# An encoder trunk on one core: x ahead in the loads, c as 48 fp32r rows, a remade opening

## The chip, the cores and the metric

The program runs on one core of a Trainium2 chip. The metric is the device time of one execution in microseconds, as the median of several runs. Engines in the profile: PE is TensorE (matmul), PEld its weight loads, DVE is VectorE, ACT is ScalarE, POOL is GpSimd, and SP issues DMAs.

## The reference

There are two layers over x (256 tokens by 1024). Each has a token mixer (grouped-query attention with axial rotary positions, three groups of dilated attention, two gates) and a squared-ReLU MLP. A vector c of 1024 values sets shift, scale and gate of both sublayers in each layer:

```
c_act = silu(c)
for l in range(2):
    ada = c_act @ w_ada[l] + b_ada[l]           # (6 * 1024): sh1 sc1 gt1 sh2 sc2 gt2
    h = rms(x, g_mix[l]) * (1 + sc1) + sh1
    parts = h @ w_in[l]                          # q, k, v of four attentions, two gates
    ...                                          # rope, attentions, branches
    x = x + gt1 * (mixed @ w_out[l])
    h2 = rms(x, g_mlp[l]) * (1 + sc2) + sh2
    x = x + gt2 * (square(relu(h2 @ w_ff1[l])) @ w_ff2[l])
```

All of it is f32. Weights come to about 180 MB in all.

## The kernel before

Each large matrix product is made from fp32r matmuls in one pass. A weight tile of 128 x 1024 (512 KB) lands in `wr`; ACT copies it, rounded to fp32r, into the first half of `w`, and DVE subtracts to give the low part (`split_next`). Activations are split likewise (`hT` and others), and three matmuls (high by high, low by high, high by low) give one product: `mm3` and `many`. A plain f32 matmul is two recorded PE instructions.

The ada vectors don't use PE. DVE multiplies a 128 x 1024 tile of the transposed `w_ada` by `c_act`, which holds silu(c) on every partition, and reduces along the row: `ada_tile`, 96 times. Bias and gain follow as small DVE instructions (`sh_sc`, `first_sh_sc`, and the first one in `gt_row`).

**How the order is set.** The program records all operations in a class `Plan`, with a cost for each. A list scheduler (`run`) places them: PE's recorded order gives the due times, the other engines work backward from these, and the scheduler picks the most urgent operation that is ready on each engine. The result is a fixed order for each engine. `CFG` holds the order of the mixers' pieces (`seq0`, `seq1`: a and b are the attentions, c a qkv chunk, u and v gates, y a branch, w one ada tile), how many ada tiles go between the MLP's pieces (`ada_f0`), and which first chunk is finished first (`post0`). Constants such as `COLD`, `FIRST` and `FETCH` model start-up and transfers.

**The opening.** SP issues c (as a zero-padded block of 128 rows with an 8 x 8 identity beside it), then in the order of `OPEN["loads"]` the first half of x (`x0`, with an identity matrix, all biases and gains and half the rotary table), `x1`, two w_ada tiles and the two first weight tiles `wx` and `wy`. `OPEN["steps"]` names the steps in PE's order: C (silu of c, then eight f32 matmuls with a broadcast column, which put c on all partitions), X (sum of squares, GpSimd's power, scaling, transposes into `xT`), T (rotary tables by matmul), A (the first shift and scale), H (the first `hT`), W (a split), M (the matmuls of k = 0 for one pair of column chunks and one half of the rows), F (warm matmuls on zeros). `plain` names the pairs done by f32 matmuls without a split of h; a weight tile whose two halves are both plain isn't split at all. `eng` says whether ACT or DVE makes each copy. After this k = 1 to 7 follow, each with two ada tiles, `hT` for that k, and 24 matmuls into the same eight PSUM banks.

The diff touches lines 32 to 64 (the constants), 240 to 680 (the planner), 745 to 840 (tiles on chip, ada) and 1586 to 1770 (the opening), and the layout of the inputs from 1824 on.

## Time and profile before

| | us |
|---|---|
| median of 3 runs | 724.97 (724.77 to 725.4) |
| the profiled execution | 725.12 |
| its span, first to last instruction | 723.3 |
| PE busy | 718.4 |
| weight loads busy | 597.2 |
| DVE busy | 587.6 |
| ACT busy | 466.3 |
| POOL busy | 69.6 |

The mean granted clock of TensorE over the span is 1.00. Matmuls are pipelined, and their ends are modelled: two neighbours overlap in the table of times, so the pace of a stretch is read from the distance of the starts, or from the count of matmuls in a stage. All operations are issued from one helper line, L721, so the groups are told apart by their tiles. In brackets behind a row stands the idle time of its engine just before it, and what ended it.

### The profile page before, as it was taken

The page shows a single profiled execution, that of the slowest core. Times are in us where ns is not written, and L with a number is a line of the kernel's source. Part 1 is how long each engine was busy: PE and PEld are TensorE (multiplying, and loading weights), DVE is VectorE, ACT ScalarE, POOL GpSimd, SP SyncE. Part 2 cuts the span into 40 slices and gives each one's busy share as a digit, 9 for nine tenths or more (in the row PEclk, how much of TensorE's full clock was granted, in tenths as well). Part 3 has the DMA queues.
Part 4 walks back from the last instruction along what each step waited for, and adds up shares of the span by engine and source line. Part 5 has one row for each costly group of instructions (what it writes and reads, how often), then busy time and mean ns, then how long its engine had stood idle before and what let it go on. Part 6 is the DMA issues. An engine that isn't in the chain of part 4 may idle for free.

```text
span 723.3 us, 10610 instructions
## 1 busy us (share of the span) xinstructions
PE 718.4 (99%) x3860; PEld 597.2 (83%) x3860; DVE 587.6 (81%) x919; ACT 466.3 (64%) x791; POOL 69.6 (10%) x60
## 2 busy tenths in 40 slices
PE   9999999999999999999999999999999999999998
PEld 6788888788888888888888888878788888888887
DVE  6999999999999986594799999797899755456643
ACT  7569678965764766653565598658848766545640
POOL 0007640000100040000032201010000000000000
PEclk9999999999999999999999999999999999999999
DMA  9998668997499997596565687967376965576101
GB/s 349 408 401 270 193 203 295 348 373 243 142 350 406 381 359 278 183 325 233 175 221 207 213 328 269 338 226 280 122 258 199 344 207 159 172 229 211 52 0 59
DMA packets 50868, 180.95 MB, mean 250 GB/s; under 512 B 5728, under 2 KB 6784, under 8 KB 50816
## 3 DMA queue, kind: packets, MB, share of 16 engines
q1 hardware_dynamic: 50816, 180.28, 70.7%
q8 instruction: 30, 0.49, 0.3%
q14 instruction: 22, 0.18, 0.1%
HBM read 178.66 MB, written 1.06 MB: 248 GB/s over the span
## 4 chain that ended last, share of the span: by engine, by line
PE 98%; DMA 1%; SPq 0%; issue 0%; DVE 0%
PE ps L721 98%; DMA wr<-in_w_y 1%; SPq L721 0%; DVE xin L721 0%
## 5 line engine op out<-in xcount | busy, mean ns | idle before, releaser
L721 DVE TENSOR_TENSOR w<-wr,w 128x1024 fp32r<-128x1024 f32 x234 | 282.3, 1229 | 44.7 <-ACT w L721 44.3
L721 ACT ACTIVATE w<-wr 128x1024 fp32r<-128x1024 f32 x234 | 241.5, 1056 | 81.8 <-PE ps L721 38.9
L721 PE MATMUL ps<-w,hT 128*128 128x512 f32 x1032 | 246.4, 395 | 0.0
L721 PEld LDWEIGHTS ps<-w,hT 128*128 128x128 f32 x1032 | 190.3, 188 | 41.5 <-DVE hT L721 1.7
L721 PE MATMUL ps<-w,hid 128*128 128x512 f32 (+1 forms) x780 | 176.0, 385 | 0.0
L721 PEld LDWEIGHTS ps<-w,hid 128*128 128x128 f32 x780 | 143.1, 188 | 28.3
L721 PE MATMUL ps<-hT,w 128*128 128x512 f32 (+1 forms) x896 | 158.5, 337 | 0.0
L721 PEld LDWEIGHTS ps<-hT,w 128*128 128x128 f32 x896 | 139.4, 190 | 18.7
L721 DVE CUSTOM_DVE_ANT_0 s2k<-wr,c_act 128x1024 bf16<-128x1024 f32 x96 | 116.1, 1227 | 0.0
L721 ACT ACTIVATE s2k<-ps 128x256 f32<-128x256 f32 (+3 forms) x108 | 45.4, 440 | 81.0 <-PE ps L721 75.3
L721 DVE TENSOR_TENSOR s2k<-ps,s2k 128x256 f32<-128x256 f32 x56 | 22.8, 419 | 32.5 <-ACT s2k L721 32.5
L721 PE MATMUL ps<-w,mT 128*128 128x512 f32 x192 | 45.6, 393 | 0.0
L721 ACT ACTIVATE s2k<-s2k 128x512 f32<-128x512 f32 (+1 forms) x62 | 38.6, 623 | 9.2 <-DVE s2k L721 8.3
L721 PEld LDWEIGHTS ps<-w,mT 128*128 128x128 f32 x192 | 35.5, 188 | 7.4 <-ACT mT L721 0.2
L721 POOL TENSOR_TENSOR rstd<-rstd,half 128x8 f32<-128x8 f32 (+1 forms) x20 | 30.1, 1509 | 87.8 <-DVE rstd L721 87.7
L721 POOL TENSOR_TENSOR ss<-ss,half 128x1 f32<-128x1 f32 x8 | 11.1, 1383 | 261.7 <-DVE ss L721 254.6
L721 DVE TENSOR_TENSOR hid<-s2k,hid 128x512 fp32r<-128x512 f32 x28 | 20.1, 719 | 19.8 <-ACT hid L721 19.7
L721 ACT ACTIVATE pr<-pr,st 128x256 f32<-128x256 f32 (+1 forms) x64 | 32.3, 558 | 0.8 <-DVE st L721 0.8
L721 DVE TENSOR_TENSOR s2k<-ps,gtb 128x512 f32<-128x512 f32 (+1 forms) x18 | 11.7, 658 | 18.4 <-PE ps L721 18.4
L721 PEld LDWEIGHTS ps<-xin,s2k 128*128 128x128 f32 x180 | 20.9, 141 | 6.3 <-DVE s2k L721 1.2
L721 PE MATMUL ps<-xin,s2k 128*128 128x128 f32 x180 | 26.0, 274 | 0.0
L721 POOL TENSOR_TENSOR s2k<-s2k,tabs 128x256 f32<-128x256 f32 (+1 forms) x20 | 20.2, 1031 | 57.8 <-ACT s2k L721 51.5
(109 smaller groups left out, 505.0 us busy)
## 6 DMA issues: line engine op xcount, KB each, us to landing
wr<-in_w_ff SPq DMA_DIRECT2D x120, 512.0 KB, 4.9
wr<-in_w_ada SPq DMA_DIRECT2D x96, 512.0 KB, 5.7
wr<-in_w_gate SPq DMA_DIRECT2D x32, 512.0 KB, 4.8
wr<-in_w_qkv SPq DMA_DIRECT2D x24, 512.0 KB, 5.3
wr<-in_w_x SPq DMA_DIRECT2D x16, 512.0 KB, 5.2
wr<-in_w_out SPq DMA_DIRECT2D x16, 512.0 KB, 5.3
wr<-in_w_y SPq DMA_DIRECT2D x8, 512.0 KB, 6.7
wr<-in_w_ba SPq DMA_DIRECT2D x8, 512.0 KB, 6.1
```

The lines of the kernel that those rows point to most:

```text
L721: getattr(self.real[o["e"]], o["op"])(*map(real, o["a"]), **{n: real(z) for n, z in o["k"].items()})
```

## The change

The loads begin with x (`x1` first, then `x0`). c is 48 rows (c and the identity at rows 0 and at 32, zeros elsewhere) and comes over ACT's DMA queue. It is rounded to fp32r by ACT into a tile `c_f`, DVE puts the low part into rows 32 to 47, and the eight matmuls become fp32r over all 128 rows; GpSimd clears the tile first. GpSimd also makes the identity matrix, which was loaded before. Biases and gains of later layers load at 50 us; those needed first come with `x1`. The reductions of the w_ada tiles take bias and gain as scalar operands, and the small DVE instructions behind them go, but for the additions of the 1 and b of the scales. In the opening only the pair x of row block 1 is plain, so both first weight tiles are split. [...]

```diff
-  post0=(5, 2, 1, 0), s2k=9, ahead=1, last="k",
+  post0=(5, 2, 0, 1), s2k=9, ahead=1, last="k",
-  ada_f0=[2, 3, 11, 2, 0, 1, 0, 8, 1], ...
+  ada_f0=[2, 4, 5, 1, 1, 3, 1, 7, 2], ...
-  seq0="w v v w a w c3 c4 a w w v w a v u a w w w w w u w w w b w b w w v w u w y w w w y w y y w".split(),
+  seq0="a w v w v w w c4 c3 a w u v w a a w v u w w w w w w b w w b u w w w v y w w y w w w y w y".split(),
...
-WARM = 5
+WARM = 8
+CR = 48
-    loads="x0 x1 a0 a1 wx wy",
-    steps="C T1 F0 X0 A X1 T0 F1 Wy H0 Wx H1 My0 Mx0 Mx1 My1",
+    loads="x1 x0 a1 a0 wy wx",
+    steps="Wy C X0 X1 T0 T1 F0 A H1 Mx1 F1 H0 Wx My0 Mx0 My1",
-    eng=dict(c0="a", c1="a", ss00="d", ss01="a", ss10="d", ss11="a", xn00="a", xn01="d", xn10="a",
-             xn11="a", xT00="a", xT01="a", xT10="d", xT11="a", ... h0="d", h1="a", i0="d", i1="a"),
-    plain="y0 y1",
+    eng=dict(c0="d", c1="d", ss00="a", ss01="a", ss10="a", ss11="a", xn00="d", xn01="a", xn10="d",
+             xn11="a", xT00="a", xT01="a", xT10="a", xT11="a", ... h0="a", h1="d", i0="a", i1="d"),
+    plain="x1",
-FILL = (6000.0, 3), (8500.0, 4)
+FILL = (6000.0, 3), (10500.0, 1)
...
+    pool.memset(ident, 0.0)
+    pool.affine_select(out=ident, in_=ident, compare_op=ALU.not_equal, fill=1.0, ...)
...
-        dve.tensor_tensor_reduce(junk, raw, c_act, 0.5, 0.0, ALU.mult, ALU.add, col)
+        dve.tensor_tensor_reduce(junk, raw, c_act, *ends(l, w, s, k), ALU.mult, ALU.add, col)
+    def ends(l, w, s, k):
+        ks = slice(k, k + 1)
+        if s < 2 and (l, w) == (0, 0):
+            return (0.5, early[:, 0, ks]) if s == 0 else (early[:, 2, ks], 0.0)
+        return (g_col[:, l, w, ks], 0.0) if s == 1 else (0.5, b_col[:, l, w, s, ks])
+    def one_more(k):
+        sc = shg[0, 0][:, 1, k : k + 1]
+        dve.tensor_tensor(sc, sc, early[:, 1, k : k + 1], op=ALU.add)
...
     with plan.first():
-        sp.dma_start(c_in, a["c"])
+        act.dma_start(c_in[:CR], a["c"])
...
     keep_warm(WARM)
+    pool.memset(f32(c_f), 0.0)
...
-        c_sig = s2k("c_sig")[:KT, :P]
-        z = c_row[:KT]
+        c_sig = s2k("c_sig")[:CR, :P]
+        z = c_row[:CR]
...
+            act.activation(c_f[:CR], c_in[:CR], AF.Copy)
+            dve.tensor_tensor(c_f[low, :P], c_row[low], f32(c_f[low, :P]), op=ALU.subtract)
...
-                    ps[:, k * P : (k + 1) * P], pick[:, kk : kk + 1].to_broadcast([P, P]), c_row,
+                    ps[:, k * P : (k + 1) * P], c_f[:, P + kk : P + kk + 1].to_broadcast([P, P]), c_f[:, :P],
...
-        for z in (h, hi):
+        for z in (hi, h):
             act.activation(z, xT[:, k, :], AF.Identity, bias=v[:, 0, k : k + 1], scale=v[:, 1, k : k + 1])
...
+            with plan.not_before(50000.0):
+                sp.dma_start(small, a["small"])
```

## Rows read from the trace of the kernel before

**Rows 1.** The page: busy time, share of the span and instructions of each engine.

```profile
PE 718.4 (99%) x3860; PEld 597.2 (83%) x3860; DVE 587.6 (81%) x919; ACT 466.3 (64%) x791; POOL 69.6 (10%) x60
```

**Rows 2.** The chain of waits: start us, duration us, what.

```profile
4.06 8.51 DMA wr<-in_w_y
...
12.70 18.07 PE ps L721 x71
...
30.81 689.44 PE ps L721 x3732
```

**Rows 3.** Stages: PE, PEld, DVE, ACT, POOL busy us (instructions), clock, DMA share, GB/s.

```profile
10.00:20.00 10.00, 9.69 (x42) 6.25 (x40) 9.47 (x21) 8.63 (x15) 0.00 (x0) 1.00 1.03 412
20.00:36.00 16.00, 15.96 (x70) 12.69 (x69) 14.91 (x27) 8.59 (x12) 0.00 (x0) 1.00 1.03 408
...
60.00:100.00 40.00, 40.00 (x210) 32.83 (x209) 39.66 (x66) 31.66 (x67) 27.38 (x24) 1.00 0.67 210
100.00:200.00 100.00, 100.00 (x635) 81.34 (x634) 96.64 (x166) 75.02 (x142) 6.22 (x6) 1.00 0.78 273
```

**Rows 4.** Timeline of SP's queue: start, duration, engine, line, operation, tiles, count.

```profile
0.74 0.38 SPq L721 DMA_DIRECT2D c_in<-in_c  x1
1.18 0.89 SPq L721 DMA_DIRECT2D xin<-in_x  x2
```

**Rows 5.** Timeline of PE in the opening; in brackets idle time and its end.

```profile
1.45 2.50 PE L721 MATMUL ps<-warm 128*128 128x512 f32 x4 [1.45 <-DVE half L721]
...
3.75 3.30 PE L721 MATMUL ps<-c_in 128*128 128x128 f32 x16
...
9.56 1.53 PE L721 MATMUL ps<-xin,s2k 128*128 128x128 f32 x12
...
12.70 1.95 PE L721 MATMUL ps<-wr,s2k 128*128 128x512 f32 x4 [0.31 <-DMA wr<-in_w_y]
14.09 3.31 PE L721 MATMUL ps<-w20wx,hT 128*128 128x512 f32 x12
17.23 1.88 PE L721 MATMUL ps<-wr,s2k 128*128 128x512 f32 x4
```

**Rows 6.** Timeline of the weight loads: an ordinary one, one behind DVE.

```profile
18.09 0.19 PEld L721 LDWEIGHTS ps<-wr,s2k 128*128 128x128 f32 x1 [0.24 <-issue]
...
30.80 4.66 PEld L721 LDWEIGHTS ps<-w,hT 128*128 128x128 f32 x21 [0.47 <-DVE hT L721]
```

**Rows 7.** Timeline of DVE in the opening.

```profile
7.45 0.69 DVE L721 CUSTOM_DVE_ANT_0 s2k<-xin 128x512 bf16<-128x512 f32 x1
...
8.99 1.22 DVE L721 CUSTOM_DVE_ANT_0 s2k<-wr,c_act 128x1024 bf16<-128x1024 f32 x1
...
12.04 0.68 DVE L721 COPY xT<-ps 128x512 f32<-128x512 f32 x1
...
16.85 0.28 DVE L721 TENSOR_SCALAR shg<-shg,xin 128x1 f32<-128x1 f32 x1
...
17.51 1.23 DVE L721 TENSOR_TENSOR w<-wr,w 128x1024 fp32r<-128x1024 f32 x1 [0.38 <-ACT w L721]
18.65 0.42 DVE L721 TENSOR_TENSOR hT<-s2k,hT 128x256 fp32r<-128x256 f32 x1
```

**Rows 8.** Timeline of ACT in the opening.

```profile
5.88 0.63 ACT L721 ACTIVATE s2k<-xin 128x512 bf16<-128x512 f32 x1 [2.98 <-DMA xin<-in_x]
...
6.51 1.17 ACT L721 ACTIVATE c_act<-ps 128x512 f32<-128x512 f32 x2
...
16.41 1.06 ACT L721 ACTIVATE w<-wr 128x1024 fp32r<-128x1024 f32 x1 [0.77 <-DMA wr<-in_w_x]
```

**Rows 9.** Groups by form: tiles, shapes, count; busy us, mean ns; idle before.

```profile
L721 PE MATMUL ps<-w,hT 128*128 128x512 f32 x1032 | 246.4, 395 | 0.0
...
L721 PE MATMUL ps<-w,hid 128*128 128x512 f32 x744 | 171.7, 390 | 0.0
...
L721 POOL TENSOR_TENSOR ss<-ss,half 128x1 f32<-128x1 f32 x8 | 11.1, 1383 | 261.7 <-DVE ss L721 254.6 <-DVE xin L721 7.1
```

## The prediction

> **What bounds the kernel now.** I read the page's busy times first: TensorE is busy 718.4 of 723.3 us [rows 1]. A busy share can hide waits, so the chain of waits comes second: from 12.70 to 720.25 us it is TensorE alone, and ahead of it stands one transfer, the first w_y tile, issued at 4.06 and landed 8.51 us later, at 12.57 [rows 2]. The stage table comes third. Between 20 and 36 us 70 matmuls fill 15.96 us, 0.228 each; from 60 to 200 us TensorE is never idle [rows 3]. Three places are left to win: the opening before TensorE runs without a gap, small delays inside the dense stream, and the number of changes between kinds of matmul in it. Fewer DVE instructions later, or a later load of the biases, lie beside a full TensorE.

> From 10 to 20 us the DMA engines are full (share 1.03, 412 GB/s), and DVE is busy 9.47 of 10 us [rows 3]. Two resources can set when TensorE becomes dense, and the later one decides.

> **The change part by part.**

> *Loads.* c leaves SP's queue for ACT's, so the first x is issued at 0.74 instead of 1.18 [rows 4]: 0.44 us. By the tile shapes 68 (c) + 776 + 640 KB stood ahead of the first w_ada tile; now it is 26 + 788 + 512, 158 KB less, at 412 GB/s 0.39 us. Every w tile of the opening lands 0.83 us earlier, the last of the first k at 11.74 instead of 12.57. The first x tile has 814 KB up to its end instead of 844 (0.07 us): 5.88 [rows 8] becomes 5.37. Should ACT's table load come ahead of the issue of c, c is later by about a microsecond, which the next point absorbs.

> *c.* Sixteen matmul passes took 3.30 us at the slow rate of the start, 0.21 each [rows 5]; eight single passes cost 1.7 there. The warm matmuls ahead of them grow from 640 to 1024 columns; at 2.3 us for 640 (1.45 to 3.75) they last until 5.1, so c ends near 6.8 instead of 7.05. What reads it is the reduction of the first w_ada tile, and that lands three tiles (512 KB, 1.27 us each at 412 GB/s) ahead of the last: 12.57 - 3.81 - 0.83 = 7.93. I cost the shorter c at nothing: that landing hides it. GpSimd clears c_f and builds the identity first, which the trace doesn't show. Nearest are its 128x1 powers, 1.38 us each [rows 9]; three instructions then take 0 to 4.2 us, from 0.4 to 4.6 at the latest, and the warm matmuls cover that. Beyond it c, and all behind it, slips by the excess. I take 1 us, since a clear does less than a power.

> *The first k on TensorE.* Four f32 matmuls (two passes of 0.43 each) and twelve fp32r ones ran from 12.70 until 17.23 + 4 x 0.43 = 18.95 [rows 5]. Now it is two and eighteen: 1.72 us become 6 x 0.227 = 1.36. With the loads TensorE could be through at 18.95 - 0.83 - 0.36 = 17.76, 1.2 us earlier.

> *DVE in the opening,* up to the shift and scale of k = 1 (17.13 before, 16.85 + 0.28 [rows 7]). Added: the low part of the first w_y tile, 1.15 (rows follow each other 0.07 closer than they last); two copies of c out of PSUM, one more scaling of x. Dropped: two sums of squares, 0.69 each, which pay for the copies (nearest row 0.68); a 0.68 copy of xT, which pays for the scaling with 0 to 0.3 to spare; the scale's fix-up of k = 0 and of k = 1, 0.28 each. Net 0.3 to 0.6 more, from a start 0.51 earlier. The bias and gain that now ride in the reductions as scalar operands have no row; I take 0, bounded by one small instruction of 0.28 each way. So the shift and scale stand at 16.9 to 17.2. Two ACT instructions that make h follow, the rounded one now first, 1.1 us, and DVE's 0.42 us low part: 18.4 to 18.7, or 18.1 without the gaps that DVE had before. It ended at 19.07, since DVE was in a weight split from 17.51 to 18.65 [rows 7]. If that happens again it is 18.9. So this side gives 0.2 to 1.0; I take 0.7, because DVE has its other operands 0.83 earlier.

> *ACT.* Added: the w_y split 1.06, two sums of squares of 0.63, a copy of xT; gone: two copies of c, 1.17, and one scaling [rows 8]. Net about 1.2, against 0.5 of earlier start and the 0.77 us that ACT stood idle before the split of k = 1's w_x at 16.41. That split starts where it did or 0.1 earlier; it was not the last to arrive.

> The latest of these is DVE: 0.7 us at k = 1.

> *Inside the dense stream.* At 30.80 a weight load stood idle 0.47 us for DVE's hT against an ordinary 0.24 [rows 6]: 0.25 us lost behind a late w_ada tile. Tiles come 0.83 earlier, TensorE 0.7, and a 0.28 us DVE step per k is gone: 0.25 won (bounds 0 and 0.5).

> *The other orders.* Both mixers' orders, post0 and the planner's rules change; the first mixer keeps its 24 w_ada tiles, the second goes from 27 to 29. Matmuls of w by hT average 0.2388 us (246.4/1032), those of w by hid 0.2308 (171.7/744) [rows 9]: 8.3 us above the plainest stream, the opening's share included. A new order can save a small part of that; a stall would be new. I take 0, bounds 1.0 won and 2.5 lost (two waits for DVE steps of 1.23).

> *Sum.* The profiled execution took 725.12 (span 723.3): 725.12 - 0.7 - 0.25 = 724.17. The median of the three runs is 724.97, 0.15 below it: 724.0. Its own range is 723.0 to 724.9.

> GpSimd's 128x1 power is issued beside a DVE reduction of two SBUF operands that runs from 7.45 for 0.69 us [rows 7], and such powers average 1.38 [rows 9]. The new x path has two of them beside reductions of 1.22.
> [...]
> From the rows, block t = 1 is ready at 5.37 + 1.6 + 0.2 + 1.38 + 0.6 + 0.5 + 0.6 = 10.3, block 0 near 12.2. TensorE needs neither before w_x lands at 11.74, and block 1's f32 matmuls cover 1.7 us more. [...]

> **Rivals.**
> 1. *More than that.* k = 1 starts when TensorE is free (1.2), the late tile costs nothing (0.25), and the new orders change kind less often (0.3 to 1). For it: every matmul above the 0.228 pace is time to be had [rows 3, 9]. Against it: DVE has no spare time before 18 us. Time 722.4 to 723.3; 22%.
> 2. *The second split eats the gain.* 1.22 on DVE and 1.06 on ACT, with the copies of c, fall just ahead of k = 1's reductions; h stands behind a split again. For it: 9.47 of 10 us of DVE [rows 3]. Against it: the tiles' 0.83. Gain 0 to 0.2: 724.7 to 725.2; 15%.
> 3. *Slower: DVE falls behind in the first mixer.* It is busy 39.66 of 40 us from 60 to 100 and 96.64 of the next 100 [rows 3]. An order that puts other DVE work ahead of what TensorE needs next costs waits of about 1.23 us; two of them outweigh the opening's 0.95. It decides once DVE's 3.7 idle us of 60 to 200 lie ahead of the attention matmuls instead of behind. Against it: the work per stage is unchanged. 726.4 to 727.5; 9%.
> 4. *Slower: the clock.* TensorE worked from 1.45 until 0.31 us before 12.70 without idling, and its passes fell from 0.21 us in c to 0.11 in the transposes [rows 5]. In the new opening it may idle while c waits for GpSimd, or between c and the transposes. [...]

> [...]

> **How the numbers follow.** Forecast 50%, rivals 22, 15, 9 and 4. About 0.2%, 1.45 us, is what a measurement of this kernel can tell from no change: below 723.5 or above 726.4. Some 15 of the forecast's 50 lie below 723.5; with rival 1 faster has 37%. Same has 35 + 15 = 50%, slower 13%. The range 722.5 to 725.6 takes in the forecast, most of rival 1 and rival 2.

> **What would show it.** TensorE's first w_x or w_y matmul near 11.8; c in eight passes and its copies on DVE; k = 1's second fp32r matmul at 17.8 to 18.5 (19.2 before); no weight load idle over 0.3 us near 30; 60 to 200 us without idle TensorE. A k = 1 after 18.9 speaks for rival 2, weight loads that wait for DVE between 60 and 200 us for rival 3, passes of 0.21 us after 7 us for rival 4. I am wrong if the dense stream from k = 1 to the end, some 704 us, changes by more than 1 us.

## The result and the profile after

The changed kernel takes 727.58 us (median of 6 runs, 725.82 to 728.46), the kernel before 724.87 beside it: ratio 1.0032, 95% interval 1.0022 to 1.0042, so slower, by 2.7 us in the medians. The forecast was 724.0, with a range up to 725.6. The runs of before lie within 0.7 us, those of after spread over 2.6, and the profile is of the fastest of them (725.82, span 724.0).

The page of after, busy times (answers to [rows 1]): TensorE has 0.7 us less work in a span that is 0.7 longer.

```profile
PE 717.7 (99%) x3854; PEld 595.0 (82%) x3854; DVE 590.6 (82%) x907; ACT 469.2 (65%) x795; POOL 69.3 (10%) x63
```

The chain of waits of after, some of its longest pieces (answers to [rows 2], same columns). Before, TensorE was the chain from 12.70 on. Now it is only from 57.61 on, and what stands ahead begins with c's transfer: 4.08 us, landed at 4.82.

```profile
0.74 4.08 DMA c_in<-in_c
...
19.34 6.73 DMA wr<-in_w_ada
...
53.24 2.35 DVE w L723 x2
...
57.61 663.29 PE ps L723 x3616
```

Timelines of GpSimd, ACT and DVE in the opening of after. GpSimd is through by 1.45, so the clear and the identity are cheap. ACT stands idle 2.38 us for c. DVE's first reduction of a w_ada tile starts at 9.21, 0.22 later than in [rows 7], and takes 1.28 instead of 1.22.

```profile
0.73 0.21 POOL L723 MEMSET c_f<- 128x136 f32 x1 [0.29 <-POOLq L1896]
...
1.16 0.29 POOL L723 TENSOR_SCALAR_AFFINE_SELECT ident<-ident 128x128 f32<-128x128 f32 x1
```

```profile
4.84 0.31 ACT L723 ACTIVATE s2k<-c_in 48x128 f32<-48x128 f32 x1 [2.38 <-DMA c_in<-in_c]
```

```profile
9.21 1.28 DVE L723 CUSTOM_DVE_ANT_0 s2k<-wr,c_act,xin 128x1024 bf16<-128x1024 f32 x1
...
18.08 1.23 DVE L723 TENSOR_TENSOR w<-wr,w 128x1024 fp32r<-128x1024 f32 x1
19.23 0.42 DVE L723 TENSOR_TENSOR hT<-s2k,hT 128x256 fp32r<-128x256 f32 x1
```

Timeline of PE in the opening of after (answers to [rows 5]). TensorE stands idle 1.04 us for c. In this run c's eight passes then follow each other at 0.11 us (0.21 in before's c).

```profile
1.45 3.76 PE L723 MATMUL ps<-warm 128*128 128x512 f32 x4 [1.45 <-DVE half L723]
6.25 1.11 PE L723 MATMUL ps<-c_f 128*128 128x128 f32 x8 [1.04 <-DVE c_f L723]
7.29 2.01 PE L723 MATMUL ps<-s2k,xin 64*128 64x128 f32 x16
...
12.87 1.88 PE L723 MATMUL ps<-wr,s2k 128*128 128x512 f32 x4
...
18.99 2.23 PE L723 MATMUL ps<-w,hT 128*128 128x512 f32 x9
```

The same view of a second run of the same, unedited kernel (e1_after, 727.71 us). c's passes and the rotary tables run at half that rate (1.97 and 3.79 us for the same counts), and k = 1 starts at 21.03 instead of 18.99 (its first pass with `w` and `hT`).

```profile
1.45 3.78 PE L723 MATMUL ps<-warm 128*128 128x512 f32 x4 [1.45 <-DVE half L723]
5.87 1.97 PE L723 MATMUL ps<-c_f 128*128 128x128 f32 x8 [0.64 <-DVE c_f L723]
7.77 3.79 PE L723 MATMUL ps<-s2k,xin 64*128 64x128 f32 x16
11.49 1.87 PE L723 MATMUL ps<-ident,s2k 128*128 128x128 f32 x8
13.19 1.03 PE L723 MATMUL ps<-warm 128*128 128x384 f32 x4
```

Stages of after (answers to [rows 3], same columns): from 10 to 20 us DVE and ACT are both full (9.81 and 9.71), and TensorE has 9.51 of 10; from 60 to 200 it is never idle, as before.

```profile
10.00:20.00 10.00, 9.51 (x43) 6.60 (x42) 9.81 (x20) 9.71 (x16) 0.90 (x1) 1.00 1.03 410
...
60.00:100.00 40.00, 40.00 (x208) 32.31 (x207) 39.93 (x67) 31.93 (x66) 25.72 (x24) 1.00 0.65 211
100.00:200.00 100.00, 100.00 (x633) 80.80 (x633) 96.30 (x163) 74.96 (x143) 6.89 (x6) 1.00 0.76 271
```

The idle weight load of 30.80 [rows 6] is gone, but a new one stands at 57.61, behind DVE:

```profile
57.61 2.37 PEld L723 LDWEIGHTS ps<-w,hT 128*128 128x128 f32 x11 [0.62 <-DVE s2k L723]
```

### The profile page after: what moved, and what is told of

Its sections match the earlier page's. It is cut to its first block, busy times and chain, and to the rows that moved or that the text cites. A ratio compares the mean times of both kernels' runs of the same rounds, so it can differ in the third digit from the quotient of the medians.

```text
span 724.0 us, 10626 instructions
## 1 busy us (share of the span) xinstructions
PE 717.7 (99%) x3854; PEld 595.0 (82%) x3854; DVE 590.6 (82%) x907; ACT 469.2 (65%) x795; POOL 69.3 (10%) x63
## 3 DMA queue, kind: packets, MB, share of 16 engines
HBM read 178.57 MB, written 1.06 MB: 248 GB/s over the span
## 4 chain that ended last, share of the span: by engine, by line
PE 92%; DVE 3%; ACT 2%; DMA 1%; issue 1%; POOL 0%; ACTq 0%; DVEq 0%
PE ps L723 92%; DVE s2k L723 2%; DMA wr<-in_w_ada 1%; DVE w L723 1%; ACT s2k L723 1%; DMA c_in<-in_c 1%; ACT hT L723 0%; ACT tabs L723 0%; ACT w L723 0%; ACT xT L723 0%; DVE rstd L723 0%; ACT w20wx L723 0%; DVE xin L723 0%; DVE c_act L723 0%; DVE shg L723 0%
## 5 line engine op out<-in xcount | busy, mean ns | idle before, releaser
L723 PEld LDWEIGHTS ps<-hT,w 128*128 128x128 f32 x896 | 139.4, 190 | 18.7
L723 DVE CUSTOM_DVE_ANT_0 s2k<-wr,c_act,small 128x1024 bf16<-128x1024 f32 x80 | 101.3, 1278 | 5.3 <-DMA wr<-in_w_ada 5.1
L723 PE MATMUL ps<-ident,s2k 128*128 128x128 f32 x180 | 26.3, 275 | 0.5 <-ACT s2k L723 0.5
L723 DVE TENSOR_TENSOR s2k<-ps,gtb 128x512 f32<-128x512 f32 (+1 forms) x18 | 11.7, 659 | 18.4 <-PE ps L723 18.3
L723 PEld LDWEIGHTS ps<-ident,s2k 128*128 128x128 f32 x180 | 20.8, 141 | 6.8 <-DVE s2k L723 2.4
```

Source lines behind the costliest of these rows:

```text
L723: getattr(self.real[o["e"]], o["op"])(*map(real, o["a"]), **{n: real(z) for n, z in o["k"].items()})
```

## Experiments

In the experiments marked *frozen* the edit is made where the finished order is issued, so every other instruction stays where it was on its engine.

**The unedited kernel twice more.**

> The changed kernel, unedited, for another profile. If the spread is the clock: a run near 727.5 has c's passes and the first tables at 0.21 us a 128-column pass (0.11 in the run at 725.82), k=1's first fp32r matmul near 20.7 (18.99) and the same length from there to TensorE's last (701.9). Rival, the spread lies in the mixers: k=1 near 19.0 and the rest longer.

> The changed kernel, unedited, one more draw: by the clock, k=1's first fp32r matmul at 18.99 plus what the run's time lies above 725.82; by the rival, k=1 near 19.0 whatever the time.

e1: 727.71 us, k = 1 at 21.03; e2: 726.72 us, k = 1 at 20.13. From k = 1 to TensorE's last matmul the three profiles have 701.89, 701.78 and 701.69 us. The spread lies in the opening, and it is the clock: the trace's first record of the full clock stands at 5.05 us in the fastest run, at 10.49 in e2 and at 13.12 in e1, and the passes change their pace there (in before's trace it stands at 6.57, where c's passes go from 0.21 to 0.11 us). (Ahead of that record the stages' clock column says 1.00 all the same; there the pace of the passes tells.) The idle time alone doesn't set it: e1's was the shorter (0.64 against 1.04).

In these three profiles of one kernel, each with TensorE idle ahead of c, 8 us lie between the earliest rise and the latest; what sets its place isn't shown.

**c back on SP's queue (frozen).**

```diff
-            for o in order:
-                getattr(self.real[o["e"]], ...
+            for o in sorted(order, key=lambda o: not (o["dma"] and o["e"] == "ACT")):
+                getattr(self.real["SP" if o["dma"] else o["e"]], ...
```

> The changed kernel with one edit: c is issued on SP's queue ahead of x again, every engine's order unchanged. Theory A (c on ACT's queue lands 2.3 us late, beside x's 788 KB, TensorE stands idle from 5.2 to 6.25 us, and when its clock rises then differs from run to run): c lands near 2.6 us, the c matmuls start at 5.2 with no idle time, the runs lie within 0.8 us of each other and the median is 725.0 to 726.2. Rival B (the loss and the spread come from the new orders later on): median 727 to 728 and a spread over 2 us, as now.

725.78 us (11 runs, 725.51 to 726.69, in two clusters with 0.6 us between them), ratio 1.0015 (1.0006 to 1.0024). That is 1.8 us off the loss. In the profile (726.47) TensorE doesn't idle in the opening, yet its passes are slow until the tables are through, and its clock rises only at 11.00:

```profile
4.25 2.59 PE L723 MATMUL ps<-c_f 128*128 128x128 f32 x8
6.82 3.79 PE L723 MATMUL ps<-s2k,xin 64*128 64x128 f32 x16
```

**Another warm matmul ahead of c; one less (both frozen).**

```diff
 pe.matmul(ps, warm[:, :128], warm[:, :512], start=True, stop=True)
-pe.matmul(ps, warm[:, :128], warm[:, :512], start=True, stop=True)   # a3
+pe.matmul(ps, warm[:, :128], warm[:, :384], start=True, stop=True)   # a2, behind both
```

> The changed kernel with one more warm matmul of 384 columns between the first two and c; c stays on ACT's queue. Theory A, the clock's part of it: TensorE isn't idle at 5.2 us, c starts 0.0 to 0.3 us later than now, the spread falls under 0.8 us and the median is 725.6 to 726.6. Rival B, or a lateness of c that costs by itself: median 727 to 728.

> The changed kernel without its second warm matmul, so that TensorE stands idle from about 3.3 to 6.25 us in every run. Theory A: the granted clock rises after c in every run, passes of c and of the tables at 0.21 us, median 727.8 to 729.5. Rival B: nothing waits for a warm matmul, 727.6 as now.

a2: 725.51 us (11 runs, 725.14 to 725.93), ratio 1.0008 (0.9999 to 1.0017). a4_no_scalars, meant for another question, came out as the same kernel, since its edit didn't reach the reductions (the trace still shows 1277 ns and the operand's tile): 725.25 (725.07 to 726.06), ratio 1.0005 (0.9996 to 1.0014). The 22 runs of a2 and a4 have a median of 725.28. a3: 727.34 (726.64 to 728.02), ratio 1.0033 (1.0021 to 1.0044), with 2.48 us idle and slow passes until 11.9 us (c's eight 1.97 us, the tables 3.79). So 384 columns of zeros take 2.3 us off the changed kernel and most of its spread (1.0 us instead of 2.6), though c's passes begin no earlier than in e1 (5.90 against 5.87). The clock rises at 4.88 in a2's profile and at 6.92 in a4's. PE of a2:

```profile
1.45 4.31 PE L723 MATMUL ps<-warm 128*128 128x512 f32 x6 [1.45 <-DVE half L723]
5.90 1.11 PE L723 MATMUL ps<-c_f 128*128 128x128 f32 x8
...
18.64 3.59 PE L723 MATMUL ps<-w,hT 128*128 128x512 f32 x15
```

> The change as in a2_warm_cover (one 384-column warm matmul ahead of c's passes), but the reductions of the w_ada tiles take the constants 0.5 and 0.0 in place of the scalar operands that carry the gain and bias rows; so gain and bias are left out of what is computed. Every engine's order stays. If the scalar operands are the dear part (1.28 us a reduction against 1.22 before): k=1's first fp32r matmul 0.2 to 0.3 us earlier than a2's 18.64, and 725.1 to 725.4. Rival, they cost nothing that the end sees and a2's remaining 0.6 us above the kernel before lies in the order of the later work: 725.5, as a2.

**The kernel before with c on ACT's queue (frozen).**

```diff
+ self.real["ACT" if o["op"] == "dma_start" and <its output is c_in> else o["e"]]
```

> The kernel before with one edit: c is issued on ACT's queue, every engine's order unchanged. Theory A: c lands at 4.5 to 5 us instead of 2.56, TensorE is idle for more than 1 us ahead of c, median 725.8 to 728, spread over 1 us. Rival B: c has time to spare, 724.9 within 0.4.

728.37 us (727.9 to 728.97), ratio 1.0047 (1.0034 to 1.006). This one part of the change, alone, makes the kernel before slower by 3.5 us. The chain and PE of b1: c is 5.26 us under way, TensorE idle 2.74 (3.95 to 6.69), c's passes slow, and the clock rises at 10.30.

```profile
0.73 5.26 DMA c_in<-in_c
```

```profile
6.69 3.76 PE L721 MATMUL ps<-c_in 128*128 128x128 f32 x16 [2.74 <-DVE c_in L721]
```

**Wide warm work behind c, with c on SP (frozen): one matmul of 512 columns (a5), two (a7).**

```diff
 # behind the last of c's eight passes
+pe.matmul(ps, warm[:, :128], warm[:, :512], start=True, stop=True)   # twice in a7
```

> The change as in a1_c_on_sp (c issued on SP's queue ahead of x), with one wide f32 warm matmul of 512 columns right behind c's passes. a1 had no idle TensorE in the opening and yet its clock rose only at 11.0 us, and its runs fell into two clusters 0.9 us apart. If the thin fp32r passes of c are what delays the rise, the wide matmul behind them gives an early rise in every run: one cluster, spread under 0.5 us, 725.6 or less. Rival, the warm matmul only delays the tables, or the two clusters come from elsewhere: two clusters again, 725.8 or more.

> The change with c on SP's queue ahead of x and two 512-column warm matmuls behind c's passes (a5_sp_then_warm has one). If wide work up to the tables settles the clock: a spread under 0.5 us around 725.0 to 725.2. Rival, a5's spread stays: 725.0 to 725.9, or later by the 0.4 to 0.9 us that the second warm matmul holds the tables back.

a5: 725.59 us (725.04 to 727.1), ratio 1.0011 (1.0002 to 1.002). a7: 725.6 (725.38 to 728.24, three of 11 above 728), ratio 1.0019 (1.0009 to 1.0029). The spread stays, so my idea that the thin passes of c hold the clock back isn't borne out. The profiled runs of a5 (725.04) and a7 (725.57) have an early rise, at 6.05 and 4.53 us; none of their late runs was profiled, so that the clock makes this spread too isn't shown. Why a1, a5 and a7 spread and the 22 runs of a2 and a4 hardly do is open.

**The scalar operands (frozen, a2 with them taken out of all 96 reductions).**

```diff
- dve.tensor_tensor_reduce(junk, raw, c_act, *ends(l, w, s, k), ...)
+ dve.tensor_tensor_reduce(junk, raw, c_act, 0.5, 0.0, ...)
```

> a2_warm_cover with the constants 0.5 and 0.0 in all 96 reductions of w_ada tiles in place of the scalar operands, so gain and bias are left out of what is computed; every engine's order stays. If the scalar operands cost what the group means differ by (1278 ns against 1227): 0.05 us a reduction on DVE, two reductions a k, and 0.1 to 0.4 us at the end, 725.0 to 725.3 against 725.51 and 725.25 in the two draws without it. Rival, DVE's 0.05 us are hidden behind TensorE: 725.25 to 725.5.

724.5 us (11 runs, 724.28 to 724.85), ratio 0.9995 (0.9986 to 1.0004). Against the 22 runs with the operands that is 0.78 us less, and no run of either reaches into the other's (the kernel before had 724.84, 724.87 and 724.90 beside a2, a4 and a6). The groups of reductions, first a2's twin with the operands, then a6 (busy us, mean ns, idle before):

```profile
L723 DVE CUSTOM_DVE_ANT_0 s2k<-wr,c_act,small 128x1024 bf16<-128x1024 f32 x80 | 101.3, 1277 | 5.5 <-DMA wr<-in_w_ada 5.5
L723 DVE CUSTOM_DVE_ANT_0 s2k<-wr,c_act,xin 128x1024 bf16<-128x1024 f32 x16 | 20.3, 1280 | 0.0
```

```profile
L723 DVE CUSTOM_DVE_ANT_0 s2k<-wr,c_act 128x1024 bf16<-128x1024 f32 x96 | 115.8, 1217 | 5.6 <-DMA wr<-in_w_ada 5.6
```

60 ns each, 5.8 us of DVE in all, of which 0.78 reach the end. It isn't a wait for the operands' later load: the idle time ahead of the reductions is the same, 5.5 and 5.6 us, and ended by w_ada tiles. The profiles have 0.13 us of it ahead of k = 1 (18.64 in a2, 18.51 in a6) and 0.59 behind. The weight load behind DVE near 57 us, which after's and a4's profiles have and a2's hasn't, isn't there either; its row in a6 runs through:

```profile
49.88 10.16 PEld L723 LDWEIGHTS ps<-w,hT 128*128 128x128 f32 x45
```

**The lists of orders.** b2 is the kernel before with the four new lists (`post0`, `ada_f0`, `seq0`, `seq1`); v1 has c on SP in the source, so that all is ordered anew; c2 and c3 are the changed kernel with the four old lists and the opening of a2 or a5; c4 is a2 with the old `seq0` alone. The edits are lines of `CFG` as in the change's diff, in b2 forward and in c2 to c4 back; v1's is

```diff
-        act.dma_start(c_in[:CR], a["c"])
+        sp.dma_start(c_in[:CR], a["c"])
```

> The kernel before with only the changed lists of orders (the opening's split order, the first layer's tile order and the two orders of the mixers), c and the loads as before. If the new orders are what costs a2 its remaining 0.6 us: 725.2 to 725.5. Rival, the orders are free and the rest lies in the opening's other parts (scalar operands, the shorter c): 724.85, as the kernel before.

> The change with c's DMA issued on SP's queue in the source, ahead of x, so that the planner orders everything anew around an early c. If c's lateness is the whole loss of the change: 724.5 to 725.0. Rival, a1's late rise of the clock and two clusters come with an early thin c here too: 725.5 to 726.7.

> The changed kernel with the 384-column warm matmul of a2_warm_cover, and all four lists of orders (split order, first layer's tile order, both mixers) as in the kernel before; the opening is that of a2. From k=7's first fp32r matmul to TensorE's last the new orders took 663.25 us in a2 and 663.65 in b2_orders, the old ones 662.48. If the orders cost that: a2's 725.51 less 0.5 to 0.8, so 724.7 to 725.0, at or a little under the kernel before. Rival, the old lists fit the new opening badly, as the new ones fitted the old opening badly in b2_orders: 725.5 to 726.5.

> As c2_old_lists, but with the opening of a5_sp_then_warm (c on SP's queue, one 512-column warm matmul behind c's passes). a5's profiled run had the earliest k=1 (18.62) and 725.04 us. If orders and opening add up: 724.3 to 724.8 in its better runs, with a5's spread of some 0.7 us above. Rival as for c2: 725.5 to 726.5.

> As a2_warm_cover, with only the order of the first layer's mixer (seq0) as in the kernel before; the second layer's stays new. In the profiles the new orders lose about 0.45 us between k=7 and the first w,oa matmul, in the first layer, and about 0.3 behind it. If the loss lies where the profiles put it: 725.1 to 725.3, between a2 and c2. Rival, the orders only work as a set: 725.5 or more.

b2 726.63 us (1.0024, 1.0015 to 1.0033); v1 728.07 (1.0038, 1.0026 to 1.0051); c2 729.2 (1.0062, 1.0048 to 1.0075); c3 728.85 (1.0056, 1.0044 to 1.0069); c4 731.16 (1.009, 1.0076 to 1.0104). Each exchange of the lists loses, in both directions, and each profile has new waits of TensorE around 57 to 65 us, as v1's has; v1's clock also rose only at 10.70 us. The weight loads of b2, v1, c2 and c4 show one wait each; by this no price can be given to the lists alone.

```profile
58.56 1.45 PEld L721 LDWEIGHTS ps<-w,hT 128*128 128x128 f32 x7 [0.73 <-DVE s2k L721]
```

```profile
59.49 1.69 PEld L723 LDWEIGHTS ps<-w,hT 128*128 128x128 f32 x8 [1.30 <-ACT w L723]
```

```profile
63.27 0.76 PEld L723 LDWEIGHTS ps<-w,hT 128*128 128x128 f32 x4 [1.48 <-ACT v L723]
```

```profile
65.23 0.76 PEld L723 LDWEIGHTS ps<-w,hT 128*128 128x128 f32 x4 [2.27 <-DVE w L723]
```

**Breaks in the dense stream (frozen).** d1 cuts groups of transposes in two by the pass that follows them, d2 (on the kernel before) and d3 (on a2) pull neighbouring groups together. One place of d1 and one of d2, in TensorE's order:

```diff
-ps<-xin,s2k 128x128 x4
+ps<-xin,s2k 128x128 x2
+ps<-w,hT 128x512
+ps<-xin,s2k 128x128 x2
-ps<-w,hT 128x512 x2
+ps<-w,hT 128x512
```

```diff
 ps<-xin,s2k 128x128 x4
+ps<-xin,s2k 128x128
 ps<-w,hT 128x512 x8
-ps<-xin,s2k 128x128
```

> The kernel before with TensorE's order alone edited: 19 groups of four or more transposes are cut in two by the 512-column pass that follows them, so there are 38 changes of kind more (19 into transposes, 19 out) and the same instructions on every engine. In the profiles a pass that follows a transpose takes 0.31 us against 0.23. If a break costs that: 19 x 0.08 to 0.10 = 1.5 to 1.9 us, so 726.4 to 726.8. Rival, the breaks cost nothing and the longer passes are only where waits are booked: 724.9.

> The kernel before with nine pairs of neighbouring groups of transposes pulled together (the 3 to 9 passes between them go behind the second group); nothing else. If a break costs 0.08 to 0.10 us and the second group's data is ready: 0.6 us less at most, 724.2 to 724.5, below both kernels. Rival, the second group is issued as soon as its data is there, and pulled ahead it waits: 724.9 to 726.

> a2_warm_cover with eleven such pairs pulled together. By the first theory 725.51 less up to 0.9, so 724.6 to 725.0; by the rival 725.5 to 727.

d1 726.2 us (1.0018, 1.0009 to 1.0026). The edit made 36 cuts, not the 19 of the expectation, so a break costs 1.29 / 36 = 0.036 us, under half of what I had read from the longer pass behind it: the transposes ahead of it are shorter by the rest (in before's trace behind 60 us, from start to start in the median, the pass behind a transpose takes 0.31 us instead of 0.23, and the transpose ahead of it 0.03 instead of 0.11). a2's three more breaks between k = 7 and the first w,oa pass are then worth 0.1 us. d2 731.62 (1.0095, 1.0081 to 1.0108) and d3 733.43 (1.0123, 1.0108 to 1.0139): the rival holds, a group is issued as soon as its data is there, and TensorE waits if it comes sooner. PE of d2:

```profile
70.77 0.33 PE L721 MATMUL ps<-xin,s2k 128*128 128x128 f32 x1 [0.99 <-DVE s2k L721]
```

## Why the prediction was wrong

The loss in medians: 727.58 - 725.28 = 2.30 us for the clock behind a late c (a2 and a4), 725.28 - 724.5 = 0.78 for the scalar operands (a6), and 724.5 - 724.87 = -0.37 for all the rest, together 2.71. The last of these is within what can be told from nothing. It holds what the dropped small DVE instructions saved, too: a6 leaves gain and bias out, so 0.78 is the price of the operands and not of that part of the change as a whole.

- *c*, the step that failed: "I cost the shorter c at nothing: that landing hides it." I asked only when c's reader needs it, and not what TensorE does until c comes. I had bounded GpSimd's clear, which ended at 1.45, and not the transfer: 26 KB issued at the same moment as 788 KB of x took 4.08 us, where 68 KB at the head of SP's queue had taken 1.82 in the trace of before. In the trace of after c's packets lie among those of x, from 2.17 to 4.23 us (48 of c, 78 of x), where before they ran by themselves, from 1.74 to 2.22. In b1, where c is issued beside x too, it took 5.26. No run has c alone on ACT's queue, so a delay of that queue's own isn't told apart from what x's packets cost. ACT's table load stands behind the issue (1.28 us from 1.18), so it didn't hold c back. TensorE then stood idle ahead of c (0.62 to 1.04 us in the three profiles), the clock's rise differed by 8 us between them (5.05 to 13.12), and the median moved by 2.3 us.
- *Rival 4* had the right mechanism and place ("it may idle while c waits"), with GpSimd as the cause in place of the transfer, at 4%; measured are 2.3 us. It didn't take passes of 0.21 us into the first k: c, the tables and the transposes behind them at half rate were enough (1.97, 3.79 and 1.87 us in e1, 1.11, 2.01 and 1.09 in the fastest run).
- *DVE in the opening*, a term mis-sized: the scalar operands "I take 0", bounded by 0.28. They are 60 ns on each of 96 reductions and 0.78 us at the end. The bound was put on one instruction, where the count was 96.
- *Loads*: right in direction. The last tile of the first k landed at 12.19 instead of 12.57 (11.83 in a2; forecast 11.74). The gain doesn't reach the first k, which begins at 12.87 (12.70 before), or 12.52 in a2: it stands behind the x path, of which the prediction said that TensorE needs it no earlier than the tiles.
- *ACT*: "it was not the last to arrive" was said of the split of k = 1's w_x. Ahead of the first k, where the sum put nothing, ACT is the last: in a2's chain of waits it is all of 8.4 to 11.3 us, right ahead of the last transposes: scaling of x, tables, a copy of xT, scaling again. GpSimd's two powers took 0.55 and 1.53 us in after's trace, against the 1.38 that the x path of the prediction had for one.

```profile
8.39 0.72 ACT s2k L723
9.11 0.97 ACT tabs L723 x2
10.08 0.49 ACT xT L723
...
10.59 0.73 ACT s2k L723
```

- *The first k* and *rival 2*: DVE's low part of k = 1's h stands behind a split again (19.23 behind 18.08 in the rows above) and ends at 19.65, in a2 at 19.31, where the prediction had 18.4 to 18.9 and before had 19.07. But DVE was not the latest any more. Before, k = 1's second pass started at 19.19, behind a weight load that waited for that low part:

```profile
19.12 11.21 PEld L721 LDWEIGHTS ps<-w,hT 128*128 128x128 f32 x50 [0.41 <-DVE hT L721]
```

Now the passes go from the first k into k = 1 every 0.227 us, and the second starts at 19.22 in the best run, 18.87 in a2 and 18.74 in a6. With c repaired 0.3 of the 0.7 came, 0.45 without the operands, and what sets it is the start of the first k.
- *Inside the dense stream*: the wait at 30.80 went, as said, and one of 0.62 at 57.61 came in the fastest run. It is gone in a6, but a2's profile has none either.
- *Other orders*: no term of their own can be shown; the opening and the lists fit only each other.
- *Rival 3* didn't happen: from 60 to 200 us TensorE has no idle time. What would have shown me wrong, a dense stream longer by over 1 us, didn't happen either. From k = 1's second pass to TensorE's last it takes 701.05 us before, 701.66 in the best run of after, 701.55 in e1, 701.35 in a2 and 700.76 in a6. Of the 2.58 us by which e1's TensorE ends later than before's, 2.07 came ahead of that pass and 0.50 behind it.

No kernel run here beats the one before with the whole computation: a2 is the best of the changed ones, equal to it within the interval.

## What to carry to other kernels

When a small load moves to a second DMA queue beside a large one, price its landing beside that load (here 4.08 us for 26 KB, against 1.82 for 68 KB ahead of it), and ask what TensorE does until then: here waits of 0.62 to 1.04 us for c came with 2.3 us in the median, and showed as a spread of 2.6 us between runs before they showed in one profile. A profile of the fastest run can hide the loss (725.82 here, the median 727.58), so take several when the times spread. And multiply a "free" operand by how often it is used (here 60 ns by 96).

## What was not expected of the hardware

```profile
63.00:65.30 2.30, 0.46 (x3) 0.07 (x1) 2.30 (x5) 2.26 (x7) 2.30 (x2) 1.00 0.21 46
65.30:66.20 0.90, 0.90 (x4) 0.77 (x5) 0.90 (x1) 0.90 (x5) 0.90 (x2) 1.00 0.87 357
66.20:69.60 3.40, 3.40 (x9) 2.59 (x9) 3.37 (x4) 1.84 (x4) 3.32 (x3) 0.50 0.87 265
```
